# Inverse square roots of a two-layer trunk: one GpSimd power instruction where eleven VectorE instructions stood

## The chip, the cores and the metric

The kernel runs on one core of a Trainium2 chip. Five engines of the core work side by side, each through its own list of instructions in a fixed order, and wait for each other by semaphores: TensorE (PE in the profile, with its weight loads apart as PEld), VectorE (DVE), ScalarE (ACT), GpSimd (POOL) and SyncE (SP), which issues most of the DMA transfers. The metric is the device time of one execution in microseconds (us). The kernel before took 2716.48 us, the median of three executions (2715.31 to 2716.92).

## The reference, cut to what matters

The input is 256 frames of 2048 features, in float32. Two layers follow each other; the first mixes frames with gated delta-net heads and band attention, the second with a Mamba-2 scan (SSD). An inverse square root stands in five places:

```python
def rms_norm(x, w):
    xf = x.astype(jnp.float32)
    y = xf * lax.rsqrt(jnp.mean(xf * xf, axis=-1, keepdims=True) + NORM_EPS)
    return (y * w.astype(jnp.float32)).astype(x.dtype)

def l2_norm(x):
    xf = x.astype(jnp.float32)
    return xf * lax.rsqrt(jnp.sum(xf * xf, axis=-1, keepdims=True) + NORM_EPS)
...
    # gated_deltanet, 8 heads of 128
    q = l2_norm(q.reshape(b_, t_, GDN_HEADS, GDN_DK)) * (GDN_DK ** -0.5)
    k = l2_norm(k.reshape(b_, t_, GDN_HEADS, GDN_DK))
...
    o = rms_norm(o, norm_w) * jax.nn.silu(z.reshape(b_, t_, GDN_HEADS, GDN_DV).astype(f32))
...
    # chunk_band_attention, 8 heads of 128
    qh = rms_norm(heads(q), q_norm_w).astype(f32) * (ATT_DH ** -0.5)
    kh = rms_norm(heads(k), k_norm_w).astype(f32)
...
    # mamba2_ssd, 8 groups of 512
    y = rms_norm(y.reshape(b_, t_, SSD_GROUPS, -1), norm_w.reshape(SSD_GROUPS, -1)).reshape(b_, t_, SSD_DINNER)
...
    # each layer
        h = rms_norm(x, norm_mix_w[layer]) * (1.0 + sc1) + sh1
        mix = ...
        x = x + g1 * mix
        h = rms_norm(x, norm_mlp_w[layer]) * (1.0 + sc2) + sh2
        x = x + g2 * sq_relu_mlp(h, mlp_w1[layer], mlp_w2[layer])
```

The scales and shifts of each layer come from a product of a vector of 2048 conditions with a matrix of 2048 by 12288.

## The kernel before, in words

**Products.** Every weight product is made from split numbers. A weight tile of 128x1024 comes by DMA (raw), ScalarE rounds it to the type that TensorE takes at full rate (wh, L317), VectorE makes the rest (wl = raw - wh, L321), and TensorE multiplies three times: u with wh, the rest of u with wh, and u with wl (all of them L308, into accumulators named pw, pg or pm). u is the activation in its two halves. So the weights set a beat of a load, a cast, a subtraction and a group of matmuls.

**Modulation.** On VectorE runs a second stream: the product for the scales and shifts, one tile of 128x2048 at a time with an accumulated sum (mraw, L439, 2.28 us each), 192 times. These tiles come by DMA and are worked on between other things, early in the program for layer 0 and later for layer 1.

**Stages.** By the trace: the head with the first weights and masks to about 41 us; the input projection, the delta-net heads and the attention to about 500; the output projection to about 588; norm and MLP of layer 0 to about 1306; norm, projections and the SSD mixer of layer 1 to about 2000; norm and MLP of layer 1 to the end. PE's waits in the first SSD stage, 1460 to 1565 us, and in the MLP are close to nothing.

**The roots.** `rsqrt` is called 22 times on small tiles: by `norm_r` (L838, the input is named nv, the result rsy, 128x2) once a norm, so four times; by `att_qk` (L1247, input ass, result ay, 128x8) four times; by `gdn_tile` for keys and queries (gss, gy, 128x8) four times; by `gdn_group` (goss, goy, 128x8) twice; by `ssd_gate` (L1465 to L1476, zs, zy, 128x2) eight times. `newton` starts from a guess made from the bits of the float (L271), halves the input (L272), and makes three steps of three instructions (L274 to L276).

**After a root.** In a norm, PE turns the two columns of the root into rows with two transposes (`norm_bc`, L314, pm<-ident,rsy). VectorE multiplies x by the scale and that row (hf, L862), ScalarE adds the shift and rounds (u, L864), VectorE makes the rest (u, L865), and the next product begins with u. In the attention VectorE multiplies the query or key tile by its roots (aq, L1250), and PE transposes the result (L314). In the SSD gate VectorE scales the gated rows (L1476 and on).

**POOL** does little: the masks in the head (L397 to L415), zeros at the edges of the convolutions (pad, L941 and L971), zeros of the work tiles of the triangular solve (gY, L1107), and twice zeros of a tile u of the attention (L1277) before a DMA loads the bias into it.

**The order** of instructions on each engine is made by a list scheduler from the order of the code, priorities and its own costs. A few instructions are pinned to the order of the code. Pieces of work that are written as generators are stepped in the background of the products, so that a change in how long one instruction is taken to last moves others far from it. Small tiles come from one ring of 32 buffers of 16 columns (`small`).

Of the kernel before, what the change touches and what calls it, by code (L numbers as in the profile page):

```python
# [9 lines left out]

F32 = mybir.dt.float32
F32R = mybir.dt.float32r
I32 = mybir.dt.int32
AF = mybir.ActivationFunctionType
ALU = mybir.AluOpType
AX = mybir.AxisListType
# [2 lines left out]
P = 128  # L19
# [93 lines left out]
class Trunk:  # L113
# [149 lines left out]
    def rsqrt(self, v, n, tag="rs"):  # L263

        y = self.small(n, tag + "y")
        self.newton(y, v, self.small(n, tag + "n"), self.small(n, tag + "t"))
        return y

    def newton(self, y, v, nv, t):
        nc = self.nc  # L270
        nc.vector.tensor_scalar(y.bitcast(I32), v.bitcast(I32), -0.5, 1597463007.0, op0=ALU.mult, op1=ALU.add)  # L271
        nc.vector.tensor_scalar(nv, v, -0.5, None, op0=ALU.mult)  # L272
        for _ in range(3):
            nc.vector.tensor_tensor(t, y, y, op=ALU.mult)  # L274
            nc.vector.tensor_tensor(t, t, nv, op=ALU.mult)
            nc.vector.scalar_tensor_tensor(y, t, 1.5, y, op0=ALU.add, op1=ALU.mult)  # L276

    def softplus(self, v, n, tag):

# [58 lines left out]
    def constants(self):  # L338
        nc = self.nc
        self.cst = self.const([P, NCOL], "cst")  # L340
        nc.scalar.dma_start(self.cst[:, :16], self.i["vec"][:, :16])
        self.ident = self.const([P, P], "ident")
        make_identity(nc, self.ident)
        c = self.cst[:, :16]
        h = self.const([P, 16], "c_h")
        cact = self.const([P, 16], "cact")
        nc.scalar.activation(cact, c, AF.Tanh, scale=0.5)
        nc.vector.tensor_scalar(h, c, 0.5, None, op0=ALU.mult)
        nc.vector.scalar_tensor_tensor(cact, cact, 1.0, h, op0=ALU.add, op1=ALU.mult)
        self.ones = self.const([P, P], "ones")  # L350
        nc.gpsimd.memset(self.ones, 1.0)

        self.crow = self.const([P, 16, P], "crow")
        for k in range(0, 16, 4):
            ps = self.pm()
            for m in range(4):
                self.tr(ps[:, m], cact[:, k + m : k + m + 1].to_broadcast([P, P]))
            nc.scalar.copy(self.crow[:, k : k + 4], ps)
        self.crow = self.crow.rearrange("p k j -> p (k j)")
        col = lambda n: self.cst[:, _AT[n]]  # L360
        self.nw = {}
        for l in range(2):
            self.nw["mix", l] = col("nmix")[:, 16 * l : 16 * l + 16]
            self.nw["mlp", l] = col("nmlp")[:, 16 * l : 16 * l + 16]
        self.modb = col("modb").rearrange("p (l v f) -> p l v f", l=2, v=6)
        self.ssd_nw = col("ssd_nw")
# [1445 lines left out]
```

## Time and profile before

| | |
|---|---|
| median of three executions | 2716.48 us (2715.31 to 2716.92) |
| profiled execution, span | 2717.6 us, 1.1 us over the median |
| PE busy | 2665.0 us, 98% |
| DVE busy | 2147.6 us, 79%, 3081 records |
| ACT busy | 1351.2 us, 50% |
| POOL busy | 24.5 us, 1%, 98 records |
| mean granted clock of PE | 0.998 |
| DMA | 680.06 MB, 250 GB/s over the span |

The profile is of one execution, which is a little longer than the median; no time of its own beside the span is given for it. Times in its rows count from the first instruction of the core. A row of a list in order of time has the start, the length, the engine, the line, the operation, what it writes and reads with partitions and elements, how many records of that kind were put together, and in brackets how long the engine had been idle and what ended the idle time. A row of waits has the waiting engine and place, what ended the wait, the sum in us, how many times, and the longest. A row of stretches has the stretch, its length, the busy time of each engine with the count of records, then the granted clock, the share of time that DMA was busy and its rate.

### The profile page before, as it was taken

To read this page: it belongs to the slowest core of one execution; us is meant where nothing else is said; L and a number is where in the kernel's file an instruction comes from. 1 tells how busy PE (TensorE), PEld (TensorE's weight loads), DVE (VectorE), ACT (ScalarE), POOL (GpSimd) and SP (SyncE) were. 2 spreads that over 40 slices of the span, in tenths; PEclk is the share of its full clock that TensorE was granted. 3 is DMA by queue.
4 is the path that set the end of the run, shared out by engine and by line. 5 is a ranking of instruction groups with operands and counts; after the bars stand their busy time and mean duration, and the time that the engine had idled before them with its cause. 6 is when DMAs were issued, how large, how long until landed. Compare 5 with 4: busy or idle time off the path is not lost.

```text
span 2717.6 us, 39677 instructions
## 1 busy us (share of the span) xinstructions
PE 2665.0 (98%) x15664; PEld 2350.4 (86%) x15664; DVE 2147.6 (79%) x3081; ACT 1351.2 (50%) x1976; POOL 24.5 (1%) x98
## 2 busy tenths in 40 slices
PE   5999999999999999999999999999999999999999
PEld 5887989888888888888888888888888888888888
DVE  7998998987888888889889876897777855555554
ACT  3444454546445354454556544665555354454452
POOL 1000000000000000000000000000000000000000
PEclk9999999999999999999999999999999999999999
DMA  9986487867899898988456665554558855555554
GB/s 341 353 325 235 172 301 272 294 241 282 322 339 328 328 336 330 333 331 307 165 185 217 217 234 200 203 185 172 196 177 293 324 201 188 188 191 193 186 192 134
DMA packets 100459, 680.06 MB, mean 250 GB/s; under 512 B 11185, under 2 KB 14513, under 8 KB 19377
## 3 DMA queue, kind: packets, MB, share of 16 engines
q1 hardware_dynamic: 95376, 669.07, 68.5%
q10 hardware_dynamic: 4896, 8.46, 1.0%
q8 instruction: 123, 2.02, 0.3%
q14 instruction: 64, 0.52, 0.1%
HBM read 675.33 MB, written 2.16 MB: 249 GB/s over the span
## 4 chain that ended last, share of the span: by engine, by line
PE 90%; DVE 6%; DMA 1%; ACT 1%; issue 1%; SPq 0%; ACTq 0%; DVEq 0%
PE pw L308 70%; PE pg L308 13%; PE pm L311 4%; PE pm L308 3%; DVE mraw L439 2%; DVE wl L321 1%; PE pm L314 1%; DMA mraw<-in_mod_dram 1%; DVE u L1592 0%; ACT wh L317 0%; DVE hf L862 0%; ACT pm L1042 0%; DMA raw<-in_w_ab_dram 0%; DMA x<-in_x_dram 0%; DVE u L865 0%
## 5 line engine op out<-in xcount | busy, mean ns | idle before, releaser
L317 ACT CAST wh<-raw 128x1024 fp32r<-128x1024 f32 x870 | 907.1, 1051 | 1031.6 <-PE pw L308 732.9
L321 DVE TENSOR_TENSOR wl<-raw,wh 128x1024 fp32r<-128x1024 f32 x870 | 1048.7, 1220 | 463.8 <-ACT wh L317 349.6
L308 PE MATMUL pw<-u,wh 128*128 128x512 f32 x5584 | 1321.6, 391 | 2.6 <-DVE pad L973 1.9
L308 PEld LDWEIGHTS pw<-u,wh 128*128 128x128 f32 x5584 | 1032.2, 188 | 208.2 <-issue 3.3
L308 PEld LDWEIGHTS pw<-u,wl 128*128 128x128 f32 x5584 | 702.3, 191 | 21.3 <-issue 2.1
L308 PE MATMUL pw<-u,wl 128*128 128x256 f32 x5584 | 714.5, 283 | 0.3 <-DVE wl L321 0.3
L439 DVE SCALAR_TENSOR_TENSOR mraw<-mraw,crow 128x2048 f32<-128x2048 f32 x192 | 438.0, 2283 | 17.8 <-DMA mraw<-in_mod_dram 17.5
L308 PE MATMUL pg<-wh,u 128*128 128x512 f32 x864 | 281.6, 397 | 0.0
L308 PEld LDWEIGHTS pg<-wh,u 128*128 128x128 f32 x864 | 161.9, 188 | 32.1 <-issue 0.5
L925 DVE SCALAR_TENSOR_TENSOR x<-pw,mod,x 128x256 f32<-128x256 f32 x352 | 161.1, 478 | 22.6 <-PE pw L308 20.3
L308 PE MATMUL pg<-wl,u 128*128 128x512 f32 x432 | 169.9, 393 | 0.7 <-DVE wl L321 0.5
L308 PE MATMUL pg<-u,wh 128*128 128x256 f32 x672 | 124.6, 285 | 0.0
L308 PEld LDWEIGHTS pg<-u,wh 128*128 128x128 f32 x672 | 105.7, 192 | 0.3
L308 PEld LDWEIGHTS pg<-wl,u 128*128 128x128 f32 x432 | 81.4, 188 | 17.6 <-DVE wl L321 2.1
L308 PE MATMUL pg<-u,wl 128*128 128x256 f32 x336 | 95.3, 284 | 0.0
L308 PE MATMUL pm<-u,wh 128*128 128x256 f32 (+1 forms) x304 | 64.6, 310 | 19.2 <-ACT wh L317 19.2
L308 PEld LDWEIGHTS pm<-u,wh 128*128 128x128 f32 x304 | 49.1, 198 | 20.3 <-ACT wh L317 20.0
L308 PEld LDWEIGHTS pg<-u,wl 128*128 128x128 f32 x336 | 64.4, 192 | 0.1
L984 DVE SCALAR_TENSOR_TENSOR u<-pad,cst,u 128x256 f32<-128x256 f32 x144 | 60.6, 477 | 3.3 <-ACT u L978 3.2
L864 ACT ACTIVATE u<-hf,mod 128x256 fp32r<-128x256 f32 x64 | 29.3, 502 | 53.0 <-DVE hf L862 53.0
L1504 ACT ACTIVATE rl<-rs 128x512 f32<-128x512 f32 x64 | 40.4, 632 | 18.9 <-DVE rs L1499 14.4
L308 PE MATMUL pm<-u,wl 128*128 128x256 f32 x176 | 46.1, 290 | 3.1 <-DVE wl L321 3.1
(299 smaller groups left out, 1580.5 us busy)
## 6 DMA issues: line engine op xcount, KB each, us to landing
raw<-in_w_dram SPq DMA_DIRECT2D x256, 1024.0 KB, 5.0
mraw<-in_mod_dram SPq DMA_DIRECT2D x192, 1024.0 KB, 6.0
raw<-in_w_ab_dram SPq DMA_DIRECT2D x56, 1024.0 KB, 5.7
raw<-in_w_ssd_dram SPq DMA_DIRECT2D x48, 1024.0 KB, 4.9
raw<-in_w_sz_dram SPq DMA_DIRECT2D x32, 1024.0 KB, 4.9
raw<-in_wo_ssd_dram SPq DMA_DIRECT2D x32, 1024.0 KB, 4.8
raw<-in_wo_ab_dram SPq DMA_DIRECT2D x16, 1024.0 KB, 5.2
sE<-sd_rowd ACTq DMA_DIRECT2D x32, 256.0 KB, 4.9
```

Source lines behind the costliest of these rows:

```text
L308: self.nc.tensor.matmul(o, a, b, start=start, stop=stop, skip_group_check=True)
L311: self.nc.tensor.matmul(o, lhsT, rhs, start=True, stop=True, skip_group_check=True)
L314: self.nc.tensor.transpose(o, a, self.ident[:k, :k])
L317: a = self.nc.scalar.copy(hi, src)
L321: b = self.nc.vector.tensor_tensor(lo, src, hi.bitcast(F32), op=ALU.subtract)
L439: x = nc.vector.scalar_tensor_tensor(raw, raw, 1.0, self.crow, op0=ALU.mult, op1=ALU.mult, accum_out=t[:, f : f + 1])
L864: nc.scalar.activation(hi, h[:, f], AF.Identity, bias=shift[:, col])
L925: nc.vector.scalar_tensor_tensor(x[:, 2 * b + f], ps[:, f, n], g[:, 2 * cb + f : 2 * cb + f + 1], x[:, 2 * b + f], op0=ALU.mult, op1=ALU.add)
L984: nc.vector.scalar_tensor_tensor(h, pad[:, f, 1 + q : 257 + q], w[:, q, j : j + 1], h, op0=ALU.mult, op1=ALU.add)
L1504: nc.scalar.activation(rl, lo, AF.Relu)
```

## The change

`rsqrt` no longer calls `newton`. It issues one GpSimd instruction, a two-input operation that raises the input to the power in a second tile. That tile is a new constant, 128x16 of -0.5, written once in `constants` by GpSimd. Each root takes one buffer of the small ring and not three. Shapes, callers and readers stay as they are.

```diff
@@ class Trunk
     def rsqrt(self, v, n, tag="rs"):
 
         y = self.small(n, tag + "y")
-        self.newton(y, v, self.small(n, tag + "n"), self.small(n, tag + "t"))
+        self.nc.gpsimd.tensor_tensor(y, v, self.power[:, :n], op=ALU.pow)
         return y
-
-    def newton(self, y, v, nv, t):
-        nc = self.nc
-        nc.vector.tensor_scalar(y.bitcast(I32), v.bitcast(I32), -0.5, 1597463007.0, op0=ALU.mult, op1=ALU.add)
-        nc.vector.tensor_scalar(nv, v, -0.5, None, op0=ALU.mult)
-        for _ in range(3):
-            nc.vector.tensor_tensor(t, y, y, op=ALU.mult)
-            nc.vector.tensor_tensor(t, t, nv, op=ALU.mult)
-            nc.vector.scalar_tensor_tensor(y, t, 1.5, y, op0=ALU.add, op1=ALU.mult)
...
         self.ones = self.const([P, P], "ones")
         nc.gpsimd.memset(self.ones, 1.0)
+        self.power = self.const([P, 16], "power")
+        nc.gpsimd.memset(self.power, -0.5)
```

DVE has 2254 entries in its list where it had 2499, POOL 126 where it had 103; ACT and SP have as many as before. Line numbers of the changed kernel are 10 lower up to about L350, and 8 lower behind that: the power is L265, nv L830, hf L854, wl L311, aq L1242, mraw L431. The order moves in three places that matter.

First VectorE at the norm ahead of the MLP of layer 0 (x4 means four alike in a row; wl is the rest of a weight tile, hf the modulated x). Before, from the end of the residual:

```order
L925 SCALAR_TENSOR_TENSOR x_82<-pw_5573,mod_125,x_82 128x256 x4
L838 TENSOR_SCALAR nv_5676<-pm_5554 128x2
L271 TENSOR_SCALAR rsy_5678<-nv_5676 128x2
L272 TENSOR_SCALAR rsn_5679<-nv_5676 128x2
L274 TENSOR_TENSOR rst_5680<-rsy_5678 128x2
...
L276 SCALAR_TENSOR_TENSOR rsy_5678<-rst_5680,rsy_5678 128x2
L321 TENSOR_TENSOR wl_5711<-raw_5708,wh_5710 128x1024
L862 SCALAR_TENSOR_TENSOR hf_5727<-x_79,mod_127,pm_5722 128x256 x2
```

And now:

```order
L917 SCALAR_TENSOR_TENSOR x_82<-pw_5443,mod_127,x_82 128x256 x4
L830 TENSOR_SCALAR nv_5546<-pm_5424 128x2
L311 TENSOR_TENSOR wl_5569<-raw_5566,wh_5568 128x1024
L854 SCALAR_TENSOR_TENSOR hf_5585<-x_79,mod_129,pm_5580 128x256 x2
L854 SCALAR_TENSOR_TENSOR hf_5612<-x_79,mod_129,pm_5580 128x256
```

The eleven steps are gone and wl follows nv at once, so that wl stands between the root's input and hf as before, but no longer behind the root.

Second VectorE at the second group of keys (gY and gX are tiles of the triangular solve, mraw the modulation's product). Before:

```order
L276 SCALAR_TENSOR_TENSOR ay_3907<-at_3909,ay_3907 128x8
L439 SCALAR_TENSOR_TENSOR mraw_4319,mod_126<-mraw_4319,crow 128x2048
L274 TENSOR_TENSOR at_3909<-ay_3907 128x8
L1108 TENSOR_TENSOR gY_3934<-pm_3929,lev_271 128x4x64
L275 TENSOR_TENSOR at_3909<-at_3909,an_3908 128x8
L1108 TENSOR_TENSOR gY_3948<-pm_3943,lev_271 128x4x64
L276 SCALAR_TENSOR_TENSOR ay_3907<-at_3909,ay_3907 128x8
...
L1250 TENSOR_TENSOR aq_3839<-aq_3839,ay_3907 128x512
L1250 TENSOR_TENSOR aq_3880<-aq_3880,ay_3907 128x512
```

And now:

```order
L1239 TENSOR_SCALAR ass_3732<-ass_3732 128x8
L439 TENSOR_TENSOR mod_128<-mod_128,cst 128x4
L311 TENSOR_TENSOR wl_3837<-raw_3834,wh_3836 128x1024
L1100 TENSOR_TENSOR gY_3750<-pm_3745,lev_257 128x8x32
L1242 TENSOR_TENSOR aq_3733<-aq_3733,ay_3801 128x512
L1100 TENSOR_TENSOR gY_3764<-pm_3759,lev_257 128x8x32
L1242 TENSOR_TENSOR aq_3774<-aq_3774,ay_3801 128x512
L431 SCALAR_TENSOR_TENSOR mraw_3946,mod_129<-mraw_3946,crow 128x2048
```

Between the root's input (ass) and the two aq stand three entries now and no mraw; the next mraw comes after both.

Third GpSimd where the delta net and the attention begin. Before:

```order
L941 MEMSET pad_2652 128x2x3
L1107 MEMSET gY_2581 128x512
L1277 MEMSET u_2573 64x4x64
L1107 MEMSET gY_2589 128x512
L941 MEMSET pad_2711 128x2x3
```

And now:

```order
L933 MEMSET pad_2594 128x2x3
L265 TENSOR_TENSOR ay_2285<-ass_2260,power 128x8
L265 TENSOR_TENSOR gy_2368<-gss_2291,power 128x8
L265 TENSOR_TENSOR gy_2383<-gss_2306,power 128x8
L265 TENSOR_TENSOR ay_2431<-ass_2337,power 128x8
L1269 MEMSET u_2515 64x4x64
L1099 MEMSET gY_2523 128x512
```

Four powers stand in one row ahead of the memsets, and the u memset has moved ahead of the first gY. On SP the DMA that loads the bias into u stands three entries earlier, ahead of two loads of weight tiles, and it now has a wait for VectorE, where it had none.

More of the change, by code (lines that the diff above doesn't have):

```diff
@@ L12 @@
 F32R = mybir.dt.float32r
-I32 = mybir.dt.int32
 AF = mybir.ActivationFunctionType
```

## The prediction

> **What bounds the kernel now.** I read the page first, then the waits of the matmul engine, then busy times by stretch. The page's busy line, its slices and its chain:
>
> ```profile
> PE 2665.0 (98%) x15664; PEld 2350.4 (86%) x15664; DVE 2147.6 (79%) x3081; ACT 1351.2 (50%) x1976; POOL 24.5 (1%) x98
> ...
> PE   5999999999999999999999999999999999999999
> PEclk9999999999999999999999999999999999999999
> ...
> PE 90%; DVE 6%; DMA 1%; ACT 1%; issue 1%; SPq 0%; ACTq 0%; DVEq 0%
> ```
>
> PE sets the end. DVE is busy 79% of the time, but its work costs only where PE waits for it. So the first question is not what 242 DVE instructions take, but which PE waits have the inverse root on their way. The waits of PE by what ended them (us in total, times, longest):
>
> ```profile
> PE pm L308 <- ACT wh L317: 19.2, 2, 17.5
> PE pm L314 <- DVE rsy L276: 7.6, 4, 6.6
> ...
> PE pm L314 <- DVE aq L1250: 2.8, 2, 2.0
> ...
> PE pm L314 <- ACT er L735: 1.8, 3, 0.6
> ...
> PE pm L314 <- DVE go L1197: 0.5, 1, 0.5
> ```
>
> The 19.2 is the start, before the first weights are there. rsy is the root of the four norms: 6.6 of its 7.6 us is one wait in the head, the other three are about 0.33 each. aq and go stand behind the roots of the attention and of the delta-net groups. The stretches (length, then busy time of PE, PEld, DVE, ACT, POOL with counts, granted clock, DMA share, GB/s):
>
> ```profile
> 0.00:28.00 28.00, 8.71 (x38) 7.91 (x38) 17.67 (x44) 8.83 (x19) 8.33 (x38) 1.00 0.91 349
> 28.00:41.00 13.00, 0.84 (x4) 0.84 (x4) 12.23 (x17) 2.77 (x6) 0.00 (x0) 1.00 0.96 349
> ...
> 240.00:500.00 260.00, 255.54 (x1717) 229.43 (x1716) 230.77 (x494) 135.44 (x358) 13.29 (x32) 0.99 0.69 244
> ...
> 582.00:612.00 30.00, 28.92 (x176) 24.38 (x175) 26.66 (x60) 17.69 (x33) 0.00 (x0) 1.00 0.33 121
> 612.00:1290.00 678.00, 678.00 (x3904) 600.37 (x3904) 577.81 (x651) 332.20 (x388) 0.00 (x0) 1.00 0.88 324
> ...
> 1460.00:1565.00 105.00, 104.90 (x513) 87.10 (x513) 93.47 (x156) 56.63 (x91) 0.21 (x2) 1.00 0.64 223
> ```
>
> The MLP has no gap at all (678.00 of 678). The first SSD stage, where four of its eight gates fall, has 0.1 us of gap. Nothing can be won there. What can be won lies in the head, at three norms, and in 240 to 500 us.
>
> **What goes and what comes.** Twenty-two roots: four norms (128x2), four of queries and keys and four of the delta net (128x8), two of its output (128x8), eight SSD gates (128x2). Each loses eleven DVE instructions of about 0.16 us, which start some 0.195 us apart where nothing stands between, so about 2 us a root. Each gains one POOL instruction, and a way from DVE to POOL and back. Call L the time from the end of the root's input to the moment a reader can start. It is 1.97 us at the norm below.
>
> **The three norms between mixer and MLP or layer** (588, 1306 and 2000 us). One of them, in order of time (start, length; in brackets the idle time before and what ended it):
>
> ```profile
> 587.82 0.16 DVE L838 TENSOR_SCALAR nv<-pm 128x2 f32<-128x2 f32 x1 [1.71 <-PE pm L308]
> 588.02 0.17 DVE L271 TENSOR_SCALAR rsy<-nv 128x2 int32<-128x2 int32 x1
> ...
> 589.38 0.39 PE L308 MATMUL pm<-u,wh 128*128 128x512 f32 x1
> 589.79 0.16 DVE L276 SCALAR_TENSOR_TENSOR rsy<-rst,rsy 128x2 f32<-128x2 f32 x1
> 589.87 1.23 DVE L321 TENSOR_TENSOR wl<-raw,wh 128x1024 fp32r<-128x1024 f32 x1
> ...
> 590.10 0.40 PE L314 MATMUL pm<-ident,rsy 128*128 128x128 f32 x2 [0.32 <-DVE rsy L276]
> ...
> 591.01 1.26 DVE L862 SCALAR_TENSOR_TENSOR hf<-x,mod,pm 128x256 f32<-128x256 f32 x3
> ...
> 592.72 0.76 PEld L308 LDWEIGHTS pw<-u,wh 128*128 128x128 f32 x4 [0.42 <-DVE u L865]
> ```
>
> PE stands 0.32 us for the root and 0.42 us for u. Between the root and hf, DVE runs one wl of 1.23 us, so hf starts late. In the new order DVE goes nv, wl, hf: wl is done while POOL works. PE has the transposes one 512-column matmul earlier, so it reaches them near 589.4.
>
> Chain after the change: pw can start at 587.98 + L + 0.15 (root's end to transposes, 589.95 to 590.10) + 0.40 (transposes) + 0.15 (hop to hf, set equal to the first) + 1.71 (hf's start to pw, 591.01 to 592.72) = 590.39 + L. PE without either wait would be there at 592.72 - 0.74 = 591.98. So the whole 0.74 is won for L up to 1.6, nothing for L = 2.3, and beyond that each microsecond of L costs one.
>
> L has two unknown parts: the power's own time, and when POOL gets its turn beside wl. No power stands in the trace. The nearest POOL rows (ns after the bar: mean of one), and one place of the head where POOL ran beside DVE:
>
> ```profile
> L941 POOL MEMSET pad<- 128x6 f32 x12 | 1.2, 102 | 238.8 <-ACT wh L317 186.2 <-DVE u L959 49.5 <-ACT aT L1306 3.1
> L397 POOL TENSOR_SCALAR Ucmask<-Ucmask 64x128 f32<-64x128 f32 x1 | 0.5, 535 | 0.0
> ...
> 4.57 0.49 DVE L348 TENSOR_SCALAR c_h<-cst 128x16 f32<-128x16 f32 x1 [4.57 <-DMA cst<-in_vec_dram]
> 4.59 1.01 POOL L408 TENSOR_SCALAR_AFFINE_SELECT lev<-lev 128x64 f32<-128x64 f32 x3
> 5.18 0.17 DVE L349 SCALAR_TENSOR_TENSOR cact<-cact,c_h 128x16 f32<-128x16 f32 x1
> ...
> 5.92 1.45 DVE L833 TENSOR_TENSOR ss<-ss,sq 128x256 f32<-128x256 f32 x3
> ...
> 6.87 0.26 POOL L408 TENSOR_SCALAR_AFFINE_SELECT lev<-lev 128x64 f32<-128x64 f32 x1
> ```
>
> Own time, from below: 0.10, the smallest memset. From above: 2.9, eleven passes of 0.26, if a power is as much work inside POOL as the eleven steps are. I take 0.3, near the 0.26 of the nearest small tile that POOL reads and writes. Turn: beside POOL, the 128x16 c_h took 0.49 where a like form alone took 0.17; a two-sided hindrance is in the rows. So I let the power wait out wl (1.2 us). L = 1.2 + 0.3 + 0.1 (hop, half the 0.2 between two DVE starts) = 1.6: just enough, **-0.74 each, -2.2 for three**. If it need not wait, L is 0.4 to 3.0, and the gain is the same for 0.3. In the Trainium skill, "SBUF — State Buffer", section "SBUF: two separate sides", the port pair that DVE and GpSimd share is an exclusive lock, held for a whole instruction when DVE reads two SBUF inputs. The c_h row agrees in direction; by that page the 1.2 us is the full rest of wl, which is the value already in the sum.
>
> **Queries and keys, delta net (240 to 500 us).** The costliest gap there is the second key. Its Newton chain started at 413.36 and was stretched to 427.07 because other DVE work was put between its steps, the last of it late:
>
> ```profile
> 413.36 0.16 DVE L271 TENSOR_SCALAR ay<-ass 128x8 int32<-128x8 int32 x1
> ...
> 423.27 2.29 DVE L439 SCALAR_TENSOR_TENSOR mraw<-mraw,crow 128x2048 f32<-128x2048 f32 x1 [2.24 <-DMA mraw<-in_mod_dram]
> ...
> 427.10 1.29 DVE L1250 TENSOR_TENSOR aq<-aq,ay 128x512 f32<-128x512 f32 x2
> ...
> 427.94 1.09 PE L314 MATMUL pm<-ident,aq 128*128 128x128 f32 x4 [2.02 <-DVE aq L1250]
> ...
> 425.70:427.90 2.20, 0.21 (x2) 0.01 (x1) 2.06 (x9) 0.00 (x0) 0.00 (x0) 0.99 0.74 209
> 427.90:431.20 3.30, 3.26 (x16) 3.29 (x17) 2.06 (x4) 1.65 (x3) 0.00 (x0) 0.50 0.97 372
> ```
>
> PE lost 2.0 us waiting, and then 3.3 us at half clock, another 1.7. In the new order both aq stand before the mraw that came late, and the root's six steps behind it are gone. **-3.7**, if no other wait of that length appears. In the Trainium skill, "TensorE: Matmul & The Clock Gate", Part 1, the clock halves only after at least one whole idle window of about 3.4 us; here 2.02 us of waiting was followed by it, so the measurement decides, and by the page alone this term would be 2.0.
>
> The other roots of the stage are read almost at once on DVE, so DVE, which is in order, stands for L (0.5 to 3.0, taken 0.6) where it worked for 2. That frees a little; nothing is booked for it, since PE's idle time in the stage is 4.5 us in all and 2.0 of it is the gap above. Its cover is 29 us of DVE idle time in 260.
>
> **SSD gates.** Alike: zs, then its reader at once. DVE is free 11.5 of 105 us, four stalls of L are 2.4 at 0.6 and 12 at 3.0. Booked at **0**. That cover is gone at the upper bound alone, and would then cost 0.5.
>
> **Head.** DVE is 12.23 of 13 busy in 28 to 41, with DMA at 0.96. Eleven steps of 0.16 free 1.8 us of DVE. Since DMA is as full, and part of the steps may have run under the tails of their neighbours, I take a third: **-0.6** (0 to -1.8). The first power starts near 15.6 and its reader hf only at 27.0, so even a very slow first one is covered here.
>
> ```profile
> 15.44 0.16 DVE L838 TENSOR_SCALAR nv<-pm 128x2 f32<-128x2 f32 x1 [4.58 <-PE pm L308]
> ...
> 27.01 0.88 DVE L862 SCALAR_TENSOR_TENSOR hf<-x,mod,R 128x256 f32<-128x256 f32 x2
> ```
>
> **Moved.** POOL now takes four powers ahead of the u memset and the first gY memsets; their inputs are all older than those memsets' need. The added memset of the constant (0.1) lies in the head on an idle POOL. On SP the bias load goes three places up, ahead of two weight loads.
>
> **Sum.** -0.6 - 2.2 - 3.7 = -6.5. The profiled execution's span is 2717.6, 1.1 over the median 2716.48; on the median's scale 2716.5 - 6.5 = **2710.0**.
>
> **The rivals.**
> (1) The gap only moves: the 240 to 500 stage is laid out anew, and a wait as long as the old one opens elsewhere in it. For it: DVE is 89% busy and DMA is late there. Against: the late mraw no longer stands ahead of a reader. Only head and norms remain, -2.8: **2713.7**, no change that can be told.
> (2) A slow power. It decides from L = 2.3, an own time of 1.0 behind wl. With 3.0 of own time L is 4.3: each norm loses 2.0 and, PE standing 3.0 us at the transposes (589.4 to 592.4), 1.7 of half clock: 3 x 3.7 = 11. Ten 128x8 roots hold DVE 1 us longer than Newton, half of it felt: +5. The second key's gain falls to about 3: **about 2729**. For it: a power is many steps. Against: 2 columns where L408 does 64 in 0.26. By the Trainium skill, "GPSIMD Engine Reference", section 2.1, the first call of newly loaded code costs about 6 us; if that came at every switch between memset and power, this rival would be dearer still. No run here shows it.
> (3) A queue is held. The bias load on SP now has a wait, for DVE, ahead of two weight loads, and DVE may itself stand for a power. It decides where that holds the loads behind it by about the time that one takes to land (last number):
>
> ```profile
> raw<-in_w_ab_dram SPq DMA_DIRECT2D x56, 1024.0 KB, 5.7
> ```
>
> A weight tile that comes 5.7 us later with PE bare gives 2716.5 + 5.7, less at most the head: **about 2722**. Against: no PE wait but the 19.2 at the start has its weights late, so some lead is there.
>
> **How the numbers follow.** Forecast 0.50, (1) 0.27, (2) 0.17, (3) 0.06. A measurement of this kernel tells 0.2%, 5.4 us, from no change, so "faster" ends at 2711.1. The forecast's own range is 2705 to 2714: by the bounds of the head (-1.8) and other small gaps of the stage (-2.5) below, by half of the 3.7 above; 0.43 of its chance is faster, 0.07 no change. Case (1) gives 0.01 faster and 0.26 no change, (2) and (3) give slower. Together 0.44, 0.33, 0.23. The range for 8 in 10 goes from 2703 to 2724, which takes in (1), (3) and the cheaper half of (2).
>
> **What would show it.** Right: the transposes after nv start within 1.6 us of its end, pw follows without the 0.42, the wait of pm for aq is under 1 us and the clock stays at 1.00 near 425. Each power shows as one POOL row under 0.6 us. Wrong: powers of over 1 us; wl or hf longer than 1.3 or 0.5 beside them; a new wait over 1.5 us between 240 and 500; raw loads issued later near 265. A time above 2717 would say that POOL's part is longer than the eleven steps it replaced.

## The result, and the profile after

The changed kernel takes 2723.73 us (median of five executions, 2721.99 to 2727.65), the kernel before 2715.49 us (five, 2713.38 to 2716.92). The ratio is 1.0033, with a 95% interval from 1.0021 to 1.0045: **slower by 8.2 us, 0.3%**. The prediction was 2710.0, faster. Its range for 8 in 10 ended at 2724, so the time lies just inside it, and on the wrong side of zero.

The page of the profile after, span and busy line:

```profile
span 2722.0 us, 39482 instructions
...
PE 2664.3 (98%) x15664; PEld 2348.9 (86%) x15664; DVE 2121.0 (78%) x2839; ACT 1351.2 (50%) x1976; POOL 58.3 (2%) x121
```

DVE has lost its 242 instructions and 26.6 us of busy time, POOL has gained 33.8 us, and PE does the same work in more time. The powers, by name (us in all and mean ns behind the first bar, then POOL's idle time before them):

```profile
L265 POOL TENSOR_TENSOR gy<-gss,power 128x8 f32<-128x8 f32 x4 | 8.5, 2130 | 7.2 <-DVE gss L1039 7.2
L265 POOL TENSOR_TENSOR rsy<-nv,power 128x2 f32<-128x2 f32 x4 | 7.5, 1876 | 964.6 <-DVE nv L830 964.6
L265 POOL TENSOR_TENSOR zy<-zs,power 128x2 f32<-128x2 f32 x8 | 7.5, 934 | 219.3 <-DVE zs L1457 219.3
L265 POOL TENSOR_TENSOR ay<-ass,power 128x8 f32<-128x8 f32 x4 | 6.6, 1638 | 29.6 <-DVE ass L1239 26.9 <-DVE mod L439 2.7
L265 POOL TENSOR_TENSOR goy<-goss,power 128x8 f32<-128x8 f32 x2 | 4.1, 2056 | 68.5 <-ACT pg L1236 37.6 <-DVE goss L1185 31.0
```

The means hide two things, the shape and a wait, which the list in order of time tells apart. A power that no long operation of DVE holds up takes 1.64 us on 128x8 and 0.69 on 128x2 (ay at 360.11 and zy at 1533.39):

```profile
360.11 1.64 POOL L265 TENSOR_TENSOR ay<-ass,power 128x8 f32<-128x8 f32 x1 [9.07 <-DVE ass L1239]
361.71 1.64 POOL L265 TENSOR_TENSOR gy<-gss,power 128x8 f32<-128x8 f32 x1
363.84 3.61 POOL L265 TENSOR_TENSOR gy<-gss,power 128x8 f32<-128x8 f32 x1 [0.49 <-DVE gss L1039]
...
595.57 1.55 POOL L265 TENSOR_TENSOR rsy<-nv,power 128x2 f32<-128x2 f32 x1 [153.87 <-DVE nv L830]
...
1533.39 0.69 POOL L265 TENSOR_TENSOR zy<-zs,power 128x2 f32<-128x2 f32 x1 [20.26 <-DVE zs L1457]
```

The longer ones stood behind a DVE operation, as the last section shows. If the time between these two shapes goes by columns, one costs (1.64 - 0.69) / 6 = 0.16 us, about as much as one instruction of the Newton steps took on DVE.

The waits of PE between 240 and 590 us, after:

```profile
PE pm L304 <- DVE go L1189: 3.5, 2, 1.9
PE pm L304 <- DVE aq L1242: 2.7, 2, 1.5
PE pw L298 <- DVE cvt L1207: 2.1, 1, 2.1
PE pm L301 <- DVE gV L1061: 1.8, 2, 1.2
PE pm L304 <- DVE gLt L1070: 1.4, 1, 1.4
```

and what DVE waited for from POOL in the same stretch:

```profile
DVE grq L1042 <- POOL gy L265: 5.3, 4, 1.8
DVE aq L1242 <- POOL ay L265: 4.0, 3, 1.5
DVE goy L1187 <- POOL goy L265: 3.3, 2, 1.8
```

Every one of the ten roots of the attention and the delta net but one has DVE standing, 12.6 us in all, and PE stands for DVE behind it. The one is that of the second key (403.01), where a wl and a gY stand between the power and its reader. The stretches, after (PE busy is the second number):

```profile
240.00:500.00 260.00, 248.59 (x1684) 222.76 (x1684) 212.30 (x366) 131.41 (x347) 32.25 (x42) 1.00 0.65 232
500.00:582.00 82.00, 79.93 (x460) 70.57 (x459) 80.93 (x112) 39.86 (x49) 0.00 (x0) 1.00 0.91 333
582.00:612.00 30.00, 29.81 (x186) 25.62 (x185) 22.33 (x40) 14.92 (x25) 1.55 (x1) 1.00 0.44 155
...
1290.00:1330.00 40.00, 39.81 (x242) 34.48 (x241) 27.54 (x47) 19.02 (x30) 1.62 (x1) 1.00 0.48 167
...
1990.00:2024.00 34.00, 33.76 (x205) 28.95 (x204) 24.66 (x45) 17.75 (x31) 1.62 (x1) 1.00 0.42 142
```

of which the last two read, before:

```profile
1290.00:1330.00 40.00, 38.91 (x234) 33.20 (x233) 31.28 (x67) 20.98 (x38) 0.00 (x0) 1.00 0.37 132
...
1990.00:2024.00 34.00, 32.88 (x196) 27.78 (x196) 28.02 (x61) 17.52 (x33) 0.00 (x0) 1.00 0.36 131
```

So two things happened. Each of the three norms gained about 0.9 us of PE time (29.81 for 28.92, 39.81 for 38.91, 33.76 for 32.88). Between 240 and 582 us PE lost 255.54 - 248.59 = 6.9 and 82.00 - 79.93 = 2.1. The norms give back 2.7 of 9.0; against a second profile of the kernel before, which the last experiment tells of, the loss is 10.7:

```profile
240.00:500.00 260.00, 257.26 (x1738) 230.82 (x1737) 234.56 (x498) 138.92 (x362) 13.32 (x32) 1.00 0.68 247
500.00:582.00 82.00, 82.00 (x480) 72.70 (x478) 75.37 (x106) 37.04 (x45) 0.00 (x0) 1.00 0.87 320
```

### The profile page after: what moved, and what is told of

It is laid out like the page before. It is cut to its first block, busy times and chain, and to the rows that moved or that the text cites. A ratio compares the mean times of both kernels' runs of the same rounds, so it can differ in the third digit from the quotient of the medians.

```text
span 2722.0 us, 39482 instructions
## 1 busy us (share of the span) xinstructions
PE 2664.3 (98%) x15664; PEld 2348.9 (86%) x15664; DVE 2121.0 (78%) x2839; ACT 1351.2 (50%) x1976; POOL 58.3 (2%) x121
## 4 chain that ended last, share of the span: by engine, by line
PE 85%; DVE 7%; issue 4%; DMA 2%; ACT 1%; POOL 1%; POOLq 0%; SPq 0%; DVEq 0%; ACTq 0%
PE pw L298 66%; PE pg L298 12%; PE pm L301 3%; PE pm L298 2%; DVE mraw L431 2%; DVE wl L311 2%; DMA mraw<-in_mod_dram 1%; PE pm L304 1%; DVE u L1584 0%; ACT wh L307 0%; DVE u L951 0%; POOL gy L265 0%; DMA raw<-in_w_ab_dram 0%; DMA x<-in_x_dram 0%; POOL ay L265 0%
## 5 line engine op out<-in xcount | busy, mean ns | idle before, releaser
L311 DVE TENSOR_TENSOR wl<-raw,wh 128x1024 fp32r<-128x1024 f32 x870 | 1050.1, 1222 | 475.3 <-ACT wh L307 358.7
L431 DVE SCALAR_TENSOR_TENSOR mraw<-mraw,crow 128x2048 f32<-128x2048 f32 x192 | 438.7, 2286 | 15.4 <-DMA mraw<-in_mod_dram 15.1
L917 DVE SCALAR_TENSOR_TENSOR x<-pw,mod,x 128x256 f32<-128x256 f32 x352 | 161.5, 480 | 22.7 <-PE pw L298 20.3
```

Of the source, the lines that this page charges most:

```text
L311: b = self.nc.vector.tensor_tensor(lo, src, hi.bitcast(F32), op=ALU.subtract)
L431: x = nc.vector.scalar_tensor_tensor(raw, raw, 1.0, self.crow, op0=ALU.mult, op1=ALU.mult, accum_out=t[:, f : f + 1])
L917: nc.vector.scalar_tensor_tensor(x[:, 2 * b + f], ps[:, f, n], g[:, 2 * cb + f : 2 * cb + f + 1], x[:, 2 * b + f], op0=ALU.mult, op1=ALU.add)
```

## The experiments

Two theories were set against each other. **A, the power's own time:** DVE works in order and stands until the power is through POOL. **B, the new order:** the scheduler has laid out the stage anew, and that costs whatever the power takes. All runs were timed against the kernel before on the same chip; the ratio of each has its 95% interval.

**A cheap operation in the same order.** A multiplication stands in for the power in all roots. The kernel leaves the inverse root out, so only its time is of use:

```diff
-        self.nc.gpsimd.tensor_tensor(y, v, self.power[:, :n], op=ALU.pow)
+        self.nc.gpsimd.tensor_tensor(y, v, self.power[:, :n], op=ALU.mult)
...
-        nc.gpsimd.memset(self.power, -0.5)
+        nc.gpsimd.memset(self.power, 1e-6)
```

> The power is replaced by a multiplication by 1e-6 on the same engine, so the roots are wrong and no work but theirs is left out; the order on every engine is that of the change, entry for entry. Only the instruction's own time is different (a 128x8 power took 1.64 us, a 128x6 memset 0.10). Theory A, the power's own time: VectorE stands for 1.64 us and two hops at ten roots between 240 and 500 us, and this makes PE's new waits; with some 1.3 us less at each, 6 to 9 of the 8.2 us come back, 2714 to 2718. Theory B, the new order: its waits stay, at least 5 of the 8.2, 2719 to 2723.

Measured: 2712.48 us, ratio 0.9988 [0.9979, 0.9997], below both ranges. The 11.3 us between this and the change are more than the whole loss. What the multiplication takes, and the stage (its rows of powers, then of stretches):

```profile
L265 POOL TENSOR_TENSOR ay<-ass,power 128x8 f32<-128x8 f32 x4 | 0.8, 202 | 30.4 <-DVE ass L1239 27.7 <-DVE mod L439 2.7
```

```profile
240.00:500.00 260.00, 255.27 (x1722) 228.22 (x1721) 221.67 (x382) 137.26 (x360) 18.37 (x42) 1.00 0.66 243
500.00:582.00 82.00, 82.00 (x481) 72.78 (x480) 76.33 (x107) 37.98 (x47) 0.00 (x0) 1.00 0.90 333
```

An instruction of 0.20 us in place of one of 1.64, in the very same order, brings PE back to 255.27 and 82.00. For the change as a whole theory A is shown: the records of TensorE, VectorE, ScalarE and GpSimd stand in the same order in both profiles. Ten roots by 1.44 us are 14.4 us; of the 11.7 between the two spans (2722.0 and 2710.3), 8.4 lie between the first and the second norm. Two of PE's waits are there with the cheap operation too (1.6 us for cvt, 0.9 for mod), so they belong to the order.

**Which roots.** `rsqrt` asks for the caller's tag; roots outside the list keep the Newton steps:

```diff
         y = self.small(n, tag + "y")
+        if tag in ('rs', 'z'):
+            self.nc.gpsimd.tensor_tensor(y, v, self.power[:, :n], op=ALU.pow)
+            return y
         self.newton(y, v, self.small(n, tag + "n"), self.small(n, tag + "t"))
         return y
```

This cut is against the kernel before, with the constant added as in the change. With `('rs', 'z')`, norms and gates:

> The power in the four norms and the eight SSD gates alone, the Newton steps in the other ten. Both theories put the loss into the ten roots between 240 and 500 us and the gain, about 1.0 us each, at three norms: 3 us under before, 2711 to 2714. If the loss comes with the norms or gates instead, 2719 or more.

Measured: 2710.93 us, 0.9981 [0.9972, 0.9990]: faster than both kernels. With `('a', 'g', 'go')`, the other ten:

> The power in the attention's and the delta net's ten roots alone. Both theories: the loss without the norms' gain, 8.2 + 3.0 over before, 2724 to 2729. A sum with the run that has the other twelve that misses the whole by over 3 us would say that a new order far away has a part.

Measured: 2728.15 us, 1.0044 [1.0031, 1.0056]. The two parts, -4.8 and +12.4 against a kernel before of 2715.76, add up to +7.6, beside 8.2 for the whole. So the loss is where it was put. With `('rs',)` alone:

> The power in the four norms alone, Newton in the gates too. The prediction booked the gates at 0, with VectorE's idle time as cover. If so this is as fast as norms and gates together: 2710 to 2712. If the gates' powers cost (the first of them took 2.60 us in the change, behind a VectorE operation), it is faster, 2707 to 2709; if they gain, 2713 to 2715.

Measured: 2710.67 us, 0.9985 [0.9976, 0.9994], 4.1 us less than the kernel before beside it. Its interval lies over that of norms and gates, so neither a cost nor a gain of the gates can be told.

**No POOL at all.** The same multiplication on VectorE, in all roots:

```diff
-        self.nc.gpsimd.tensor_tensor(y, v, self.power[:, :n], op=ALU.pow)
+        self.nc.vector.tensor_tensor(y, v, self.power[:, :n], op=ALU.mult)
```

> One multiplication by 1e-6 on VectorE in place of each root: wrong roots, no Newton steps, no trip to GpSimd; the order is laid out anew again. Theory A: no wait for GpSimd, so the forecast's gain, 2706 to 2712. Theory B: a new order of that stage costs some us by itself, 2714 to 2722.

Measured: 2710.16 us, 0.9980 [0.9971, 0.9988]. A root that cost nothing to speak of and no trip is worth 5.6 us here, in an order of its own. The power in the norms alone gets 4.1 of them.

**The ten roots in two groups.** The list is `('rs', 'z', 'a')`, so that the attention has the power and the delta net Newton:

> The power in norms, gates and the attention's four roots; Newton in the delta net's six. The power's own time costs where VectorE stands for it and PE has no other work: the attention has 4.0 us of such VectorE waits in the change, the delta net 5.3 + 3.3. If the loss of 12.4 us goes by these waits, the attention has 4 of it: 2713 to 2717. If it is the attention alone (its readers are followed at once by PE's transposes), 2722; if none of it, 2711.

Measured: 2720.86 us, 1.0019 [1.0010, 1.0028]. And `('rs', 'z', 'g', 'go')`:

> The power in norms, gates and the delta net's six roots; Newton in the attention's four. By the waits of VectorE the delta net has 8 of the 12.4 us: 2717 to 2721. If the two parts add up, this run and the one with the attention lie together as far over the run with norms and gates alone (2710.9) as the whole change does, some 13 us.

Measured: 2723.77 us, 1.0026 [1.0015, 1.0038]. Both lie above the ranges that went by VectorE's waits (2713 to 2717, and 2717 to 2721), and the expectation that the parts add up was wrong. Over the run with norms and gates alone they cost 9.9 and 12.8 us, together 22.7, where the change with both costs 12.8. The waits of PE alone would not have told why, so each of the two was run once more in its own order, entry for entry, with a cheap operation in place of the powers in question:

```diff
-            self.nc.gpsimd.tensor_tensor(y, v, self.power[:, :n], op=ALU.pow)
+            self.nc.gpsimd.tensor_tensor(y, v, self.power[:, :n], op=ALU.mult if tag == 'a' else ALU.pow)
```

> The order of the run with all but the delta net, entry for entry, with the power of the attention's four roots replaced by a multiplication by -0.5 on the same engine (wrong roots there, no other work left out). The two parts of the stage cost 9.9 and 12.9 us apart over the run with norms and gates alone, and 12.8 together, so they do not add up. Theory A, own time in a chain that both share: this comes back to 2711 to 2714. Theory B, a new order has its own cost, which here hides in the sum: it stays at 2717 to 2721.

Measured: 2718.69 us, 1.0009 [1.0000, 1.0018].

```diff
-            self.nc.gpsimd.tensor_tensor(y, v, self.power[:, :n], op=ALU.pow)
+            self.nc.gpsimd.tensor_tensor(y, v, self.power[:, :n], op=ALU.mult if tag in ('g', 'go') else ALU.pow)
...
-        nc.gpsimd.memset(self.power, -0.5)
+        nc.gpsimd.memset(self.power, 1e-6)
```

> The order of the run with all but the attention, entry for entry, with the power of the delta net's six roots replaced by a multiplication by 1e-6 (the remaining powers have the exponent 1e-6 too, so all twelve give 1; Newton stays in the attention). Theory A: 2711 to 2715. Theory B: 2718 to 2724.

Measured: 2713.75 us, 0.9992 [0.9983, 1.0000]. The exponent 1e-6 holds for the powers of norms and gates too; a gate's still takes 0.69 us. The two answers differ. With the power in the delta net, 10.0 of the 12.8 us are the power's own time and 2.8 the order. With it in the attention alone, only 2.2 of 9.9 go with the power's own time, with intervals that overlap, and 7.8 stay with a cheap operation: there theory B holds for most of the cost. One stretch where it stays, for that run and for the one with the cheap operation in all roots:

```profile
330.00:420.00 90.00, 86.21 (x519) 73.42 (x517) 83.11 (x154) 45.75 (x131) 6.65 (x14) 1.00 0.83 306
```

```profile
330.00:420.00 90.00, 89.15 (x584) 77.76 (x584) 79.28 (x128) 48.19 (x135) 10.33 (x17) 1.00 0.73 272
```

PE is 2.9 us less busy there in the first, with no power in it to wait for; the two runs are 6.2 us apart in time, so this is a part of it. What in that order costs the time was not settled: the waits of PE between 330 and 420 us name the solve's gY (1.7 us), a wl (1.3), aq (0.5) and go (0.3), and no single one carries it. In the change itself the order costs little: the cheap operation in all roots is 1.6 us over the run with norms and gates alone, with intervals that overlap.

**One step later.** After each of the ten roots a `yield`, so that the reader comes one background step later:

```diff
         r = self.rsqrt(v, 8, "a")
+        yield
         for t in range(2):
             nc.vector.tensor_tensor(a[t], a[t], self.bc(r[:, t * 4 : t * 4 + 4]), op=ALU.mult)
```

and the same behind the roots of `gdn_tile` and `gdn_group`.

> The change with one step of the background work between the power and its readers in attention and delta net, so that the two delta-net powers of a group are issued before the first is read. Theory A: VectorE waits once where it waited twice, about 2 us at two places; 2718 to 2722. If the wait behind other VectorE work was the cost, no gain: 2722 to 2725.

Measured: 2720.87 us, 1.0020 [1.0011, 1.0029], 2.9 us less than the change. That is within what was expected of theory A, but the intervals of the two ratios overlap and the order moves with the edit, so no gain of the pairing is shown. VectorE still stands 11.9 us for powers in this stretch, where it stood 12.6. One step was not enough: PE still waits for go (4.0 us) and gV (3.2).

**The norm's power twice.** As with norms and gates alone, and in the norms:

```diff
             self.nc.gpsimd.tensor_tensor(y, v, self.power[:, :n], op=ALU.pow)
+            if tag == "rs":
+                self.nc.gpsimd.tensor_tensor(y, v, self.power[:, :n], op=ALU.pow)
```

> As the run with norms and gates alone, but the power of each norm is issued twice with the same result, so that L at a norm grows by the 0.69 us that a 128x2 power takes, from 1.7 to 2.4. The prediction's rule, pw at 590.4 + L against 591.98, has the gain gone at L = 2.3: 2713 to 2716, some 3 us more than with one power. If PE has more room there than that, 2710 to 2712.

Measured: 2712.68 us, 0.9987 [0.9978, 0.9996], 1.75 us more than with one, between the two ranges and with intervals that overlap. The order of the other engines is the same in both, and the place reads, in order of time:

```profile
584.33 0.16 DVE L845 TENSOR_SCALAR nv<-pm 128x2 f32<-128x2 f32 x1 [1.73 <-PE pm L313]
584.63 1.55 POOL L267 TENSOR_TENSOR rsy<-nv,power 128x2 f32<-128x2 f32 x1 [152.58 <-DVE nv L845]
586.26 0.69 POOL L269 TENSOR_TENSOR rsy<-nv,power 128x2 f32<-128x2 f32 x1
...
587.01 0.43 PE L319 MATMUL pm<-ident,rsy 128*128 128x128 f32 x2 [0.96 <-POOL rsy L269]
```

0.69 us more at three norms would be 2.1; 1.75 was measured. The profiles tell more than the times. The stretch of this norm, with one power and with two:

```profile
582.00:612.00 30.00, 29.79 (x177) 24.97 (x176) 26.07 (x50) 18.15 (x34) 1.56 (x1) 1.00 0.40 144
```

```profile
582.00:612.00 30.00, 29.02 (x173) 24.36 (x172) 25.79 (x49) 17.39 (x33) 2.24 (x2) 1.00 0.38 138
```

L goes from 1.70 to 2.46 (584.49 to 586.95), and PE loses 0.77 here, 0.77 and 0.75 at the two other norms. So the rule that beyond some L each microsecond costs one is borne out, with an end a little later than 2.3: at 2.46 a gain of 0.1 is left against the 28.92 of the kernel before. That this kernel is still 3.0 us faster than before (1.1 to 6.0 by its interval) does not come from these three norms, and was not located.

**The kernel before once more,** without an edit.

> The kernel before once more, for a second profile of it. The first had a span of 2717.6 us, over the median, with 2.0 us of waiting for aq and 3.3 us at half clock behind it. If both belong to the order, they are there again; if the half clock is this execution's alone, the clock stays at 1.00 between 420 and 440, and the span is 1 to 3 us less.

Measured: 2716.07 us, 0.9997 [0.9987, 1.0007], span 2713.7. The place of the second key, in order of time, and the stretch:

```profile
421.20 2.27 DVE L439 SCALAR_TENSOR_TENSOR mraw<-mraw,crow 128x2048 f32<-128x2048 f32 x1
...
425.02 1.29 DVE L1250 TENSOR_TENSOR aq<-aq,ay 128x512 f32<-128x512 f32 x2
...
426.00 0.60 PE L314 MATMUL pm<-ident,aq 128*128 128x128 f32 x4
```

```profile
420.00:430.00 10.00, 10.00 (x90) 10.00 (x89) 9.79 (x18) 4.56 (x7) 0.00 (x0) 1.00 0.93 346
```

The mraw comes two microseconds earlier, without a wait for its DMA, aq follows, PE does not stand before these transposes, and the clock stays at 1.00. The same stretch of the first profile:

```profile
420.00:430.00 10.00, 7.98 (x62) 7.80 (x61) 7.15 (x16) 3.16 (x5) 0.00 (x0) 0.89 0.89 319
```

The gap and the half clock on which 3.7 us of the prediction rested are in one of the two executions, so the kernel's order does not bring them by itself. The spans of the two profiles differ by 3.9 us, and 3.6 of them lie between the first and the second norm.

## Why the prediction was right or wrong

**The norms: right in place, near in size.** "-0.74 each, -2.2 for three". PE gained 0.9 at each, where the term had two waits of 0.74; the stretch had 1.08 us without PE work before (30 - 28.92) and has 0.19 now. The norms alone are worth 4.1 us in the timed runs (1.6 to 6.5 by the interval), of which 2.7 are seen there; the rest was not located. In the trace the transposes follow nv's end (595.43) by 1.75 us, where L + 0.15 was put at 1.75, and the wait of pw for u is gone:

```profile
595.27 0.16 DVE L830 TENSOR_SCALAR nv<-pm 128x2 f32<-128x2 f32 x1 [1.73 <-PE pm L298]
595.35 1.23 DVE L311 TENSOR_TENSOR wl<-raw,wh 128x1024 fp32r<-128x1024 f32 x1
595.57 1.55 POOL L265 TENSOR_TENSOR rsy<-nv,power 128x2 f32<-128x2 f32 x1 [153.87 <-DVE nv L830]
...
597.18 0.43 PE L304 MATMUL pm<-ident,rsy 128*128 128x128 f32 x2 [0.19 <-POOL rsy L265]
```

The size of L came out right from parts of which two were off in opposite ways: the power takes 0.69, not 0.3, and it had to wait for wl less than the 1.2 assumed, since it could be issued only 0.22 us after wl began. That it would wait out wl came true, but one row that the prediction read for it does not say so: the 0.17 us of cact (5.18) were not alone. An L408 of POOL ran beside it from 4.99 to 5.35, as one had beside c_h.

**The second key: wrong.** "-3.7, if no other wait of that length appears." The second profile has no such gap to win back. The step that failed is the reading of the gap as a property of the order. The profiled execution had a span of 2717.6 us where the second one has 2713.7; that it was over the median of the timed runs was told, and not used as a warning.

**The other roots of the stage: wrong, and the cause of the sign.** "DVE, which is in order, stands for L (0.5 to 3.0, taken 0.6) where it worked for 2. That frees a little; nothing is booked for it". The own time of a 128x8 power was taken as 0.3 and is 1.64, well inside the bounds of 0.10 and 2.9, so L there is not 0.6 but 1.8 where the power is not held up, and 2.7 to 3.7 where it stands behind a wl, a pass of mraw or another power. The shorter value makes L only about as long as Newton's, and there lies the second mistake: equal length is not equal cost. The eleven steps could have other DVE work put between them, and had: an mraw and two gY stand between those of the second key in the order shown ahead of the prediction. At nine of the ten roots the power's reader stands so close behind its input in the order that DVE idles. The term was put at 0; the ten alone measured +12.4. By the profiles the sum is -2.7 at the norms, nothing at the second key and +10.7 in the stage, together +8.0, beside +8.2 measured.

**The nearest rival** was the slow power, given 0.17 and 2729. Its price for the ten roots, +5, was too low, since it counted only what L is longer than Newton's; its price for the norms, +11, was for a 128x2 power of 3.0 us. A power of 128x8 takes longer than one of 128x2, and I had one value for both shapes. The rival of the gap that only moves is true in its way: new waits did open in the stage, but several of them, up to 2.1 us each, and together more than the old one. The held queue did not decide anything: the waits of PE name no late weight load in the stage of the change.

**Gates and head.** No run speaks against the gates at 0: the norms alone are as fast as norms and gates, within the noise. The head's -0.6 can't be told from the noise of a profile; its power took 2.71 us, of which the pass beside it explains 2.0, and the cover of 11 us held.

**The size of the range.** It reached 2724 by the bound on the power, but that the time lies inside is in part luck: the rival that leads there had +11 at the norms, which gained, and +5 at the ten roots, which cost 12.4. The forecast's own range, 2705 to 2714, is also wider than the terms named for it, which give 2706 to 2712. The chance of 0.23 for slower was too small, given that the own time of the one new instruction was known only to a factor of 29.

## What to carry to other kernels

An operation that moves from a busy in-order engine to an idle one saves instructions, but it turns work into waiting unless other work stands between the sender and the reader. Count the latency of the trip where the reader follows at once, and keep the move where the order has a long operation to put into the gap: here the norms, with their wl, gained, and of the ten other roots, which lost together, only the one with a wl left DVE without a stop. Before a gap in a trace is booked as gain, see it in a second execution; and where an order is changed, run it once with a cheap instruction in the same order, since that parts the instruction's time from the order's.

## What the runs showed of the hardware that was not expected

**The power's time grows with the columns.** It is 0.69 us for 128x2 and 1.64 for 128x8, each the same within 0.02 in all roots that were not held up; a multiplication takes 0.20 for either shape. The "GPSIMD Engine Reference" of the Trainium skill, section 2.1, gives about 6 us for the first call of newly loaded code; the first power here took 2.71 us, all but 0.6 of it beside a DVE pass, so no such cost showed:

```profile
15.80 2.29 DVE L431 SCALAR_TENSOR_TENSOR mraw<-mraw,crow 128x2048 f32<-128x2048 f32 x1
15.96 2.71 POOL L265 TENSOR_TENSOR rsy<-nv,power 128x2 f32<-128x2 f32 x1 [7.12 <-DVE nv L830]
```

**A power waits out a DVE operation with two inputs in SBUF that began before it.** SBUF is the core's memory outside TensorE's accumulators. Beside this pass (end 18.09) the power ended 0.58 us later; at a norm, wl ended at 596.58 and the power 0.54 later. Both agree with a whole 0.69 that began some 0.1 us before the end of the DVE record. In the delta net it cost 2 us of 3.61:

```profile
363.67 2.28 DVE L431 SCALAR_TENSOR_TENSOR mraw<-mraw,crow 128x2048 f32<-128x2048 f32 x1
363.84 3.61 POOL L265 TENSOR_TENSOR gy<-gss,power 128x8 f32<-128x8 f32 x1 [0.49 <-DVE gss L1039]
```

The pass ended at 365.95, and the power 1.50 us behind it. An operation with one input in TensorE's accumulators did not hold a power up: beside an aq<-pg,u of 245.30 to 245.99, the power that began at 245.48 took 1.65. "SBUF — State Buffer" of the Trainium skill, section "SBUF: two separate sides", says that the one which comes first has the shared port for its whole instruction and the other is shut out. The rows agree where DVE comes first, and differ where the power does: the wl of these rows, with both inputs in SBUF, began under a running power and took its usual 1.23 us:

```profile
403.01 1.64 POOL L265 TENSOR_TENSOR ay<-ass,power 128x8 f32<-128x8 f32 x1 [2.74 <-DVE mod L439]
...
403.30 1.23 DVE L311 TENSOR_TENSOR wl<-raw,wh 128x1024 fp32r<-128x1024 f32 x1 [0.30 <-ACT wh L307]
```

With the cheap operation the wait behind DVE is there too (a multiplication of 0.20 us beside mraw took 2.17) and the kernel is fast all the same, so this wait by itself does not make the kernel slow:

```profile
358.42 2.17 POOL L265 TENSOR_TENSOR gy<-gss,power 128x8 f32<-128x8 f32 x1 [1.30 <-DVE gss L1039]
```

**After the same wait the clock halves in some executions and not in others.** Each of the fourteen profiles has one wait of PE of 1.9 to 2.2 us that begins between 1370 and 1387 us. In eight of them, both of the kernel before and that of the change among them, 3.4 us at a granted clock of 0.50 begin within 1.4 us of its end; in the other six none do. The change, and the cheap operation in the same order:

```profile
1383.00:1393.00 10.00, 8.09 (x36) 6.32 (x34) 7.40 (x19) 5.49 (x9) 0.10 (x1) 0.83 0.38 133
```

```profile
1374.00:1384.00 10.00, 8.17 (x49) 7.02 (x50) 8.98 (x22) 5.50 (x8) 0.10 (x1) 1.00 0.33 117
```

So the half clock that the prediction priced at 1.7 us is not a cost that a wait of 2 us brings each time. About 1.7 of the 11.7 us between the spans of these two kernels lie here and not at the power. What decides whether the clock halves was not settled.
